# Adding the recurrence's intra-chunk output once per pair of heads instead of after each of the last two steps

## The chip, the cores and the metric

The kernel runs on one core of a Trainium2 chip. A core has a matrix engine (TensorE; the profile writes PE for its matmuls and PEld for its weight loads, which run beside them), a vector engine (VectorE, DVE), a scalar engine (ScalarE, ACT), GpSimd (POOL) and a queue engine for transfers (SP). Matmuls write to PSUM, a small memory of eight banks per partition, each of 512 float32 values; VectorE and ScalarE read it from there into SBUF, the large on-chip memory. The metric is the device time of one execution in microseconds; less is better.

## The reference, cut to what matters

The program is one layer of a hybrid encoder for two sequences of 256 tokens each, 2048 wide: a projection, eight heads of neighbourhood attention, eight heads of a bidirectional gated delta rule, an output projection, a gated MLP and norms. The change lies in the delta rule's recurrence. For one direction and chunks of 64 tokens it is:

```python
def step(S, inp):
    q_i, k_i, u_i, w_i, g_i, qk_i = inp
    v_new = u_i - jnp.einsum('bhcd,bhde->bhce', w_i, S)
    o = jnp.einsum('bhcd,bhde->bhce', q_i * jnp.exp(g_i)[..., None], S) \
        + jnp.einsum('bhcs,bhse->bhce', qk_i, v_new)
    g_last = g_i[..., -1]
    S = S * jnp.exp(g_last)[..., None, None] + jnp.einsum(
        'bhcd,bhce->bhde', k_i * jnp.exp(g_last[..., None] - g_i)[..., None], v_new)
    return S, o
...
o = o_fwd + o_bwd
o = o * lax.rsqrt(jnp.mean(o * o, axis=-1, keepdims=True) + RMS_EPS) * norm_w.astype(jnp.float32)
o = o * jax.nn.silu(heads(z).astype(jnp.float32))
```

So a chunk's output has two summands: the state part (the query times the state S) and the part inside the chunk (`qk_i` times `v_new`). Four chunks follow each other in each direction, and the outputs of both directions are added.

## The kernel before

**Stages.** The 512 tokens of both sequences go through together, with features on the 128 partitions. First the kernel computes the projections head by head: GEMM tiles of 128 columns by 512 tokens, each in two halves (`half_gemm`), each half with a weight tile of 128x1024 that is loaded by SP's queue and split in two by `split` (`w_hi` on ScalarE, line 138, `w_lo` on VectorE, line 139). One half is 24 matmuls. Then come the output projection, and the MLP as blocks of smaller products (`block`, from line 1090), which take more than half of the time, and the last norm.

**Chains beside the GEMM stream.** Attention and recurrence are written as Python generators and stand in the lists `chains` and `side`. Within a `half_gemm`, `pump()` is called after every two k-slices (six matmuls) and drives the first generator of each list to its next `yield`. A chain thus puts its few matmuls into the GEMM stream at fixed places; `pause(n)` leaves n such places empty, so that other engines have time.

**What sets the order.** All TensorE instructions are pinned in the order in which the program issues them (`mm` and `transpose`, lines 86 to 90), and so are some others (`pin`). The order of the rest on VectorE, ScalarE and the queues is laid out by the framework's planner, by priority, which follows the place in the program; `tc.high_priority(offset=AHEAD)` moves the weights' splits 120 places forward. The framework also sets all waits between engines. Each engine works through its own queue in order.

**The recurrence.** Heads go in pairs. `recur_pair(h)` waits for both heads' preparation, takes two PSUM tiles `O[0]` and `O[1]` (one bank each, tags o0 and o1), and drives `recur(h, O)` and `recur(h + 1, O)` in turns through `together`: at each place in the stream both heads do the same piece, head h first. `O[hf]` is seen as (i, q, e): head of the pair, one of two positions `pp`, and 128 features; its partitions are two halves of 64, one for each sequence. Both heads of a pair, and both positions, therefore lie in the same two tiles.

**The four steps.** A head's loop over `st` (line 796) takes one chunk in each direction per step: the chunks at position `pp` = 0 in steps 0 and 3, at `pp` = 1 in steps 1 and 2. A step consists of
- from step 1 on: the state's products with key and query (line 811, into `pks`), the right side `rv` on VectorE (line 815), and the state part of the output, scaled, into the SBUF tile `os_` (line 820 on VectorE in step 2, line 822 on ScalarE in steps 1 and 3);
- the solve (line 827) and its copy `n` (line 829, ScalarE);
- up to step 2: the new state, products at line 838 into `pS`, then scaled and added up by VectorE (line 849), or copied by ScalarE in step 0 (line 843);
- the part inside the chunk: four matmuls into `O[0]` and `O[1]` (line 855; the trace shows them as ps_o, eight records per head). They accumulate over the two steps with the same `pp`, so that `O` is complete for `pp` = 1 behind step 2 and for `pp` = 0 behind step 3;
- in steps 2 and 3: VectorE adds `O` to `os_`, one add of 128x128 for each of the two tiles (line 860).

**The end of a pair.** `recur_pair` appends `finish_pair(h)` to `side`. Its squares (line 881, eight per pair on ScalarE, each with a row sum) read `os_`; small operations on VectorE make the norm's factor from them (lines 885 to 887), four multiplications scale `os_` (line 891), and after `FIN_GAP` = 5 places TensorE transposes `os_` (line 902; recorded in the helper's line 90 as ps_s<-ident,os). VectorE then multiplies by the gate (line 908), and `split` writes `dmix`, the output projection's input.

**The next pair.** `prepare` of the next pair waits until both heads are in `traced`, fetches their arrays (`fetch`: a load of `kq` on SP's queue and four of `uq` on POOL's, into buffers that the earlier pair's ps_o matmuls have read), and transposes `kq` and `v` through PSUM tiles of a ring of three (`sm_tile`); ScalarE's copy at line 781 (`dvn`) and VectorE's products at line 786 (`kd`) make these free.

Of the kernel before, what the change touches and what calls it, by code (L numbers as in the profile page):

```python
# [13 lines left out]
ALU = mybir.AluOpType  # L14
# [60 lines left out]
def hybrid_encoder(ctx: ExitStack, tc: tile.TileContext, xT, w_in, w_ba, w_out, w_gate,  # L75
# [4 lines left out]
    tt = nc.vector.tensor_tensor  # L80
# [5 lines left out]
    def mm(*a, **k):  # L86
        pin(nc.tensor.matmul(*a, **k))  # L87

    def transpose(*a):
        pin(nc.tensor.transpose(*a))  # L90
# [67 lines left out]
    def newton_rsqrt(out, x, pool):  # L158

        a = pool.tile(list(x.shape), F32, tag="nw", bufs=2, name="nw")  # L160
        ai, oi = a.bitcast(I32), out.bitcast(I32)
        ts(ai, x.bitcast(I32), 1, None, ALU.logical_shift_right)
        ts(oi, ai, -1, 0x5f3759df, ALU.mult, ALU.add)
        for _ in range(3):
            stt(a, out, -0.5, x, ALU.mult, ALU.mult)
            tt(a, a, out, ALU.mult)
            stt(out, a, 1.5, out, ALU.add, ALU.mult)
# [20 lines left out]
    def together(*gens):  # L188

        gens = list(gens)  # L190
        while gens:
            turn = gens[:]
            while turn:
                said = [(g, next(g, DONE)) for g in turn]
                gens = [g for g in gens if (g, DONE) not in said]
                turn = [g for g, v in said if v == LEVEL]
            if gens:
                yield

    def pause(n):  # L200
        for _ in range(n):
            yield
# [36 lines left out]
    def sm_tile():  # L239
        return psm.tile([P, T], F32, tag="s", name="ps_s")  # L240
# [101 lines left out]
    def ranged(ap, pp):  # L342

        a = ap.rearrange("p (b c t) -> p b c t", b=NB, c=4)
        return a[:, :, 0:4:3] if pp == 0 else a[:, :, 1:3]
# [405 lines left out]
    prepared, outputs, gate, traced, finished = {}, {}, {}, set(), set()  # L751
# [39 lines left out]
    def recur(h, O):  # L791
        dr = state["dr"]
        uq, kq, vn, kd = prepared[h]
        os_ = na.tile([P, 2, NB, P], F32, tag="bias", bufs=2, name="os")
        S = None
        for st in range(4):
            pp = 0 if st in (0, 3) else 1

            dirs = (0, 1) if st < 2 else (1, 0)
            if S is None:  # L800
                rv = vn[:, :, pp]
            else:
                yield from pause(S_GAP)

                pks = sm_tile().rearrange("p (w b e) -> p w b e", w=2, b=NB)
                for w in range(2):
                    for hf in range(2):
                        for b in range(NB):
                            c0 = b * L + pp * P + hf * C
                            to = pks[half[b], 1, hf] if w else pks[half[hf], 0, b]  # L810
                            mm(to, kq[:, w, c0:c0 + C], S[:, dirs[hf], b], start=True, stop=True)
                l0 = h * NB
                rv = dr.tile([P, NB, P], F32, tag=f"r{h % 2}", name="r")
                for b in range(NB):
                    stt(rv[:, b], pks[:, 0, b], egk[:, st, l0 + b:l0 + b + 1], vn[:, b, pp],
                        ALU.mult, ALU.add)
                for hf in range(2):
                    eq = egq[:, LN[hf, st] // 16, h:h + 1]
                    if st == 2:
                        stt(os_[:, pp, hf], pks[:, 1, hf], eq, os_[:, pp, hf], ALU.mult, ALU.add)  # L820
                    else:
                        act(out=os_[:, pp, hf], in_=pks[:, 1, hf], func=AF.Copy, scale=eq)
                yield from pause(R_GAP)
            pn = sm_tile()
            pn3 = pn.rearrange("p (w b e) -> p w b e", w=2, b=NB)[:, 0]
            for b in range(NB):
                mm(pn3[:, b], uq[b][:, st, 0], rv[:, b], start=True, stop=True)
            n = dr.tile([P, NB, P], F32, tag=f"n{h % 2}", name="n")
            nc.scalar.copy(n, pn3)
            yield from pause(N_GAP)  # L830
            if st < 3:
                pS = [None, None]
                for hf in range(2):
                    t = sm_tile() if hf else pg.tile([P, T], F32, tag="g", name="ps_s")
                    pS[dirs[hf]] = t[:, :2 * P].rearrange("p (b e) -> p b e", b=NB)
                for b in range(NB):
                    for hf in range(2):
                        mm(pS[dirs[hf]][:, b], kd[half[hf], st, b], n[half[hf], b],
                           start=True, stop=True)
                Sn = dr.tile([P, 2, NB, P], F32, tag=f"S{h % 2}", bufs=2, name="S")  # L840
                if S is None:
                    for d in range(2):
                        nc.scalar.copy(Sn[:, d], pS[d])
                else:
                    for d in range(2):
                        ch = st if d == 0 else 3 - st
                        for b in range(NB):
                            lane = d * 64 + ch * 16 + h * NB + b
                            stt(Sn[:, d, b], S[:, d, b], egl[:, lane:lane + 1], pS[d][:, b],  # L849
                                ALU.mult, ALU.add)  # L850
                S = Sn
                yield LEVEL
            for b in range(NB):
                for hf in range(2):
                    mm(O[hf][half[b], h % 2, pp], uq[b][half[hf], st, 1, hf * C:hf * C + C],
                       n[half[hf], b], start=(st == 0 and h % 2 == 0), stop=(st > 1),
                       skip_group_check=True)
            if st > 1:
                for hf in range(2):
                    tt(os_[:, pp, hf], os_[:, pp, hf], O[hf][:, h % 2, pp], ALU.add)  # L860
        traced.add(h)
        outputs[h] = os_

    def recur_pair(h):
        while not {h, h + 1} <= set(prepared):
            yield
        yield from pause(CORE_START)
        O = [pso.tile([P, T], F32, tag=f"o{hf}", name="ps_o")
             .rearrange("p (i q e) -> p i q e", i=2, q=2) for hf in range(2)]
        yield from together(recur(h, O), recur(h + 1, O))  # L870
        side.append(finish_pair(h))

    def finish_pair(h):
        dr, dmix = state["dr"], state["dmix"]

        ssq = dr.tile([P, 2, 2, NB], F32, tag="ssq", bufs=2, name="ssq")
        yo = na.tile([P, T], F32, tag="pT", name="yo")
        for i in range(2):
            for pp in (1, 0):
                for hf in range(2):  # L880
                    act(out=yo[:, :P], in_=outputs[h + i][:, pp, hf], func=AF.Square,
                        scale=rqs[:, pp, hf, h + i:h + i + 1], accum_out=ssq[:, i, pp, hf:hf + 1])
        yield
        rs = dr.tile([P, 2, 2, NB], F32, tag="rs", bufs=2, name="rs_o")
        ts(ssq, ssq, 1.0 / P, EPS, ALU.mult, ALU.add)
        newton_rsqrt(rs, ssq, dr)
        tt(ssq, rs, rqs[:, :, :, h:h + 2].rearrange("p q f i -> p i q f"), ALU.mult)
        for i in range(2):
            for pp in (1, 0):
                os_ = outputs[h + i]  # L890
                tt(os_[:, pp], os_[:, pp], ssq[:, i, pp, :, None].broadcast_to([P, NB, P]),
                   ALU.mult)
        yield from pause(FIN_GAP)
        while h + 1 not in gate:
            yield
        pos = []
        for i in range(2):
            po = sm_tile()
            to = po.rearrange("p (b q f c) -> p q f b c", b=NB, q=2, f=2)
            for pp in range(2):  # L900
                for hf in range(2):
                    transpose(to[:, pp, hf], outputs[h + i][:, pp, hf], ident)
            pos.append(po.rearrange("p (b q t) -> p b q t", b=NB, q=2))
        for i in range(2):
            if i:
                yo = na.tile([P, T], F32, tag="pT", name="yo")
            for pp in range(2):
                tt(ranged(yo, pp), pos[i][:, :, pp].rearrange("p b (c t) -> p b c t", c=2),
                   ranged(gate[h + i], pp), ALU.mult)
            split(dmix[:, 0, h + i], dmix[:, 1, h + i], yo, dnw)  # L910
            finished.add(h + i)
# [76 lines left out]
    st = st_cm.__enter__()  # L988
# [475 lines left out]
```

## Time and profile before

| | |
|---|---|
| runs | 2266.14, 2270.9, 2271.24 us; median 2270.9 us |
| profiled execution | 2266.53 us; its span 2264.7 us |
| busy in the span | PE 2240.1 us, DVE 1777.8 us, ACT 1031.8 us, POOL 236.6 us |
| mean granted TensorE clock | 0.997 of full speed |
| chain that ended last | PE 93%, DVE 4%, DMA 1%, issue 1% |
| the added line 860 | 32 adds of 128x128, first at 567.7 us, last at 787.9 us |
| transfers | 381.21 MB, mean 168 GB/s |

The profile is taken by the hardware on one execution, in microseconds from the start of the span. A group's row gives line, engine, operation, output<-inputs, shapes and count, then the busy time in us and the mean time of one in ns, then the engine's idle time ahead of the group and what ended it. A row of the order of time gives start, duration, line, operation and count, with the idle time ahead of it and what ended that in brackets; instructions of one kind that stand together are merged, and the count is that of all. A row of the list of waits gives who waited for whom, the sum in us, how often, and the longest. Matmuls overlap, and their ends are modelled, so the start of the next weight load tells more of the pace than a matmul's duration. "issue" is idle time for which the profile shows no releaser. A wait for several things is put down to the one that came last.

### The profile page before, as it was taken

What the parts mean: (1) busy time and instruction counts of PE and PEld (TensorE: products, weight loads), DVE (VectorE), ACT (ScalarE), POOL (GpSimd) and SP (SyncE); (2) the same over time, 40 slices, a digit from 0 to 9 for tenths busy, and PEclk for the clock granted to TensorE, in tenths of its full rate; (3) what the DMA queues carried; (4) which work ended last, traced back from release to release, by engine and by line L of the source; (5) the groups of instructions that cost most, each with busy time, mean ns of one, the idle gap of its engine ahead of it and who ended that gap; (6) DMA issues with size and microseconds to landing.
All of it is one profiled execution on the core that took longest, in us unless ns stands there. A gap on an engine that the chain in (4) does not pass through costs nothing.

```text
span 2264.7 us, 32764 instructions
## 1 busy us (share of the span) xinstructions
PE 2240.1 (99%) x12436; PEld 1914.7 (85%) x12436; DVE 1777.8 (79%) x2742; ACT 1031.8 (46%) x1552; POOL 236.6 (10%) x370
## 2 busy tenths in 40 slices
PE   9999999999999999999999999999999999999998
PEld 7888888888777788888888888888888888888888
DVE  7954799964555546898888888888888798998966
ACT  6564433333433425654444444444444464444435
POOL 1321000010000010101111110110110001001010
PEclk9999999999999999999999999999999999999999
DMA  5344322263333455777777777777777477667672
GB/s 209 130 139 149 109 98 94 100 154 117 103 103 94 178 184 177 214 196 203 206 187 211 198 214 203 207 196 210 198 192 195 143 195 198 177 180 203 181 204 84
DMA packets 112542, 381.21 MB, mean 168 GB/s; under 512 B 14049, under 2 KB 14641, under 8 KB 112129
## 3 DMA queue, kind: packets, MB, share of 16 engines
q1 hardware_dynamic: 77552, 266.25, 35.0%
q0 software_dynamic: 33680, 110.78, 23.4%
q8 instruction: 98, 1.61, 0.3%
q10 hardware_dynamic: 1152, 2.10, 0.3%
q14 instruction: 60, 0.48, 0.1%
HBM read 343.66 MB, written 35.41 MB: 167 GB/s over the span
## 4 chain that ended last, share of the span: by engine, by line
PE 93%; DVE 4%; DMA 1%; issue 1%; ACT 0%; POOL 0%; SPq 0%; DVEq 0%; ACTq 0%; POOLq 0%
PE ps_g L87 35%; PE ps_c L87 14%; PE ps_d L87 14%; PE ps_a L87 14%; PE ps_b L87 7%; PE ps_s L87 7%; DVE prod L590 1%; PE ps_s L90 1%; DVE w_lo L139 1%; DVE W L592 1%; DMA kkq<-s_gram 1%; PE ps_o L87 0%; PE ps_e L87 0%; DVE cacc L357 0%; DVE S L849 0%
## 5 line engine op out<-in xcount | busy, mean ns | idle before, releaser
L87 PE MATMUL ps_g<-xhi,w_hi 128*128 128x512 f32 x880 | 353.0, 401 | 0.0
L87 PE MATMUL ps_g<-xhi,w_lo 128*128 128x512 f32 x880 | 344.2, 391 | 0.7 <-DVE w_lo L139 0.7
L87 PE MATMUL ps_g<-xlo,w_hi 128*128 128x512 f32 x880 | 344.2, 391 | 0.3 <-DVE xlo L257 0.3
L138 ACT ACTIVATE w_hi<-w_raw 128x1024 fp32r<-128x1024 f32 x164 | 173.4, 1058 | 280.5 <-PE ps_g L87 219.9
L138 ACT ACTIVATE w_hi<-b 128x1024 fp32r<-128x1024 f32 (+1 forms) x180 | 185.8, 1032 | 239.0 <-issue 120.0
L139 DVE TENSOR_TENSOR w_lo<-w_raw,w_hi 128x1024 fp32r<-128x1024 f32 x164 | 200.1, 1220 | 110.5 <-ACT w_hi L138 103.6
L138 ACT ACTIVATE w_hi<-w_first 128x1024 fp32r<-128x1024 f32 (+1 forms) x180 | 185.4, 1030 | 180.3 <-PE ps_c L87 90.8
L139 DVE TENSOR_TENSOR w_lo<-w_first,w_hi 128x1024 fp32r<-128x1024 f32 (+1 forms) x180 | 213.6, 1187 | 59.9 <-ACT w_hi L138 56.3
L139 DVE TENSOR_TENSOR w_lo<-b,w_hi 128x1024 fp32r<-128x1024 f32 (+1 forms) x180 | 212.9, 1183 | 7.7 <-ACT w_hi L138 7.2
L87 PEld LDWEIGHTS ps_g<-xhi,w_hi 128*128 128x128 f32 x880 | 166.0, 189 | 38.3 <-issue 5.3
L87 PEld LDWEIGHTS ps_g<-xhi,w_lo 128*128 128x128 f32 x880 | 165.9, 189 | 37.1 <-DVE w_lo L139 1.1
L87 PEld LDWEIGHTS ps_g<-xlo,w_hi 128*128 128x128 f32 x880 | 166.2, 189 | 33.6 <-DVE xlo L257 1.1
L87 PE MATMUL ps_d<-xc,w_hi 128*128 128x512 f32 x704 | 175.1, 391 | 0.0
L87 PE MATMUL ps_c<-xc,w_hi 128*128 128x512 f32 x704 | 175.1, 391 | 0.0
L87 PE MATMUL ps_a<-xc,w_hi 128*128 128x512 f32 x696 | 173.1, 391 | 0.0
L87 PEld LDWEIGHTS ps_c<-xc,w_hi 128*128 128x128 f32 x704 | 129.4, 188 | 25.0
L87 PEld LDWEIGHTS ps_d<-xc,w_hi 128*128 128x128 f32 x704 | 129.3, 188 | 25.0
L87 PEld LDWEIGHTS ps_a<-xc,w_hi 128*128 128x128 f32 x696 | 127.9, 188 | 24.8
L138 ACT ACTIVATE w_hi<-w_second 128x1024 fp32r<-128x1024 f32 (+1 forms) x60 | 62.0, 1034 | 92.9 <-DVE ga L1158 50.3
L87 PE MATMUL ps_d<-xc,w_lo 128*128 128x256 f32 x704 | 98.5, 283 | 0.0
L87 PE MATMUL ps_c<-xc,w_lo 128*128 128x256 f32 x704 | 98.5, 283 | 0.0
L87 PE MATMUL ps_a<-xc,w_lo 128*128 128x256 f32 x696 | 97.4, 283 | 0.0
(391 smaller groups left out, 4199.2 us busy)
## 6 DMA issues: line engine op xcount, KB each, us to landing
w_raw<-in_w_in_dram SPq DMA_DIRECT2D x108, 512.0 KB, 3.3
b<-in_w_gate_dram SPq DMA_DIRECT2D x66, 512.0 KB, 4.1
b<-in_w_up_dram SPq DMA_DIRECT2D x66, 512.0 KB, 4.9
b<-in_w_group_dram SPq DMA_DIRECT2D x48, 448.0 KB, 4.2
w_raw<-in_w_out_dram SPq DMA_DIRECT2D x32, 512.0 KB, 3.5
w_raw<-in_w_down_dram SPq DMA_DIRECT2D x24, 512.0 KB, 3.7
w_second<-in_w_gate_dram SPq DMA_DIRECT2D x22, 512.0 KB, 7.3
w_first<-in_w_gate_dram SPq DMA_DIRECT2D x22, 512.0 KB, 4.6
```

The source lines that it names most:

```text
L87: pin(nc.tensor.matmul(*a, **k))
L90: pin(nc.tensor.transpose(*a))
L138: act(out=hi, in_=src, func=AF.Copy)
L139: tt(lo, src, r32(hi), ALU.subtract)
L590: stt(pv, W[:, s0:s1, s0:c], ndm[:, c:c + 1], kkq[:, c, 0, None, s0:c].broadcast_to([P, n, j]), ALU.mult, ALU.mult)
L592: nc.vector.tensor_reduce(W[:, s0:s1, c], pv, AX.X, ALU.add)
```

## The change

The adds at line 860 leave the loop. `recur_pair` does them behind `together`, once both heads have done all four steps: one add for each head and tile, over both positions, so four of 128x256 per pair instead of eight of 128x128. What is computed stays the same, and so do the matmuls with their order, their accumulation flags, and all places at which a generator yields.

```diff
@@ -855,9 +855,6 @@
                     mm(O[hf][half[b], h % 2, pp], uq[b][half[hf], st, 1, hf * C:hf * C + C],
                        n[half[hf], b], start=(st == 0 and h % 2 == 0), stop=(st > 1),
                        skip_group_check=True)
-            if st > 1:
-                for hf in range(2):
-                    tt(os_[:, pp, hf], os_[:, pp, hf], O[hf][:, h % 2, pp], ALU.add)
         traced.add(h)
         outputs[h] = os_
 
@@ -868,6 +865,10 @@
         O = [pso.tile([P, T], F32, tag=f"o{hf}", name="ps_o")
              .rearrange("p (i q e) -> p i q e", i=2, q=2) for hf in range(2)]
         yield from together(recur(h, O), recur(h + 1, O))
+        for i in range(2):
+            for hf in range(2):
+                os_ = outputs[h + i][:, :, hf]
+                tt(os_, os_, O[hf][:, i], ALU.add)
         side.append(finish_pair(h))
 
     def finish_pair(h):
```

## The prediction

> **What bounds the kernel now.** I read the page first (span, busy times), then the two halves of TensorE's wait list, then the group row of the added line, then the busy times by stage.
>
> ```profile
> span 2264.7 us, 32764 instructions
> PE 2240.1 (99%) x12436; PEld 1914.7 (85%) x12436; DVE 1777.8 (79%) x2742; ACT 1031.8 (46%) x1552; POOL 236.6 (10%) x370
> ```
> ```profile
> PE ps_o L87 <- DVE os L860: 11.9, 9, 3.0
> ...
> PE ps_d L87 <- DVE p L1145: 0.5, 1, 0.5
> ```
> ```profile
> PEld ps_o L87 <- DVE os L860: 10.2, 5, 3.2
> ```
> ```profile
> L860 DVE TENSOR_TENSOR os<-os,ps_o 128x128 f32<-128x128 f32 x32 | 7.9, 282 | 10.1 <-PE ps_o L87 10.1
> ```
> ```profile
> 520.00:800.00 280.00, 268.06 (x1867) 216.98 (x1866) 152.21 (x364) 102.18 (x230) 18.50 (x28) 0.99 0.37 117
> ...
> 950.00:2200.00 1250.00, 1249.52 (x7012) 1095.96 (x7011) 1088.67 (x1442) 586.94 (x715) 124.51 (x157) 1.00 0.72 196
> ```
>
> In the last fence the columns are the stretch, its length, the busy time of PE, PEld, DVE, ACT and POOL, the granted clock, the DMA share and GB/s. TensorE is busy 2240.1 of 2264.7 us, so only about 25 us of the span can be won by taking waits away. Almost half of that is one kind of wait: TensorE stands at the recurrence's output matmuls (ps_o) until the add of line 860 is done. The recurrence runs between 520 and 800 us, and that is the stretch where TensorE isn't full (268.06 of 280). Behind it, in the FFN stage, PE is full (1249.52 of 1250), so what is won there should arrive at the end.
>
> The two wait rows, 11.9 us for matmuls and 10.2 us for weight loads, are two views of the same stalls and aren't added. To size a stall I go to the order of time on the weight-load side (start, duration, name, count, and in brackets the idle time before it). The first row is a step without an add, the others the second head's half of the eight steps with one (four pairs, steps 2 and 3).
>
> ```profile
> 551.39 0.43 PEld L87 LDWEIGHTS ps_o<-n,uq 64*64 64x64 f32 x16
> ...
> 568.03 0.40 PEld L87 LDWEIGHTS ps_o<-n,uq 64*64 64x64 f32 x8 [1.85 <-DVE os L860]
> ...
> 582.45 0.34 PEld L87 LDWEIGHTS ps_o<-n,uq 64*64 64x64 f32 x8 [0.75 <-issue]
> ...
> 640.91 0.40 PEld L87 LDWEIGHTS ps_o<-n,uq 64*64 64x64 f32 x8 [3.24 <-DVE os L860]
> ...
> 656.92 0.34 PEld L87 LDWEIGHTS ps_o<-n,uq 64*64 64x64 f32 x8 [0.75 <-ACT dvT L361]
> ...
> 706.58 0.49 PEld L87 LDWEIGHTS ps_o<-n,uq 64*64 64x64 f32 x8 [2.65 <-DVE os L860]
> ...
> 723.19 0.19 PEld L87 LDWEIGHTS ps_o<-n,uq 64*64 64x64 f32 x2 [1.59 <-issue]
> 723.99 0.20 PEld L87 LDWEIGHTS ps_o<-n,uq 64*64 64x64 f32 x6 [0.61 <-DVE os L860]
> ...
> 772.72 0.40 PEld L87 LDWEIGHTS ps_o<-n,uq 64*64 64x64 f32 x8 [1.85 <-DVE os L860]
> ...
> 787.10 0.33 PEld L87 LDWEIGHTS ps_o<-n,uq 64*64 64x64 f32 x8 [0.70 <-issue]
> ```
>
> Both heads of a pair write into the same two PSUM tiles, O[0] and O[1]. Without an add, both heads' loads run through in 0.43 us. With one, the second head's loads wait until the vector engine has read the first head's part of the tile, although the columns differ: the dependency goes by the tile. At 640.91 the add itself was late, since it stood in VectorE's queue behind the state update and a weight split.
>
> **The change part by part.** *Removed: the add between the two heads.* Both heads finish in the same turn of `together`, so the 16 loads of a step now stand in TensorE's order with no reader between them, as in the row of 551.39. Each stall is worth its idle time, plus what the second half takes above 0.21 us (half of 0.43), since it also waits for the second tile's add. By row: 1.85+0.19, 0.75+0.13, 3.24+0.19, 0.75+0.13, 2.65+0.28, 1.59+0.61+0.18, 1.85+0.19 and 0.70+0.12 make 15.4 us. Where a row names "issue" or dvT as the releaser I still count it: the step has the same order, and the 0.75 us are about what an add of 0.28 us needs with the matmul before it and the way back.
>
> *Removed with it: a slower TensorE behind the longest stalls.* The chain of waits shows the 18 GEMM matmuls that follow the output matmuls:
>
> ```profile
> 568.68 4.31 PE ps_g L87 x18
> ...
> 641.55 5.90 PE ps_g L87 x18
> ...
> 707.48 5.40 PE ps_g L87 x18
> ```
> ```profile
> 642.00:646.00 4.00, 4.00 (x13) 3.13 (x12) 0.08 (x1) 0.00 (x0) 0.00 (x0) 0.64 0.32 116
> ```
>
> Behind the stalls of 3.24 and 2.65 us the same 18 matmuls take 5.90 and 5.40 us in place of 4.31, and the granted clock in 642 to 646 is 0.64. Behind a stall of 1.85 us nothing of that is seen. That is 1.59 + 1.09 = 2.7 us more, so the stalls are worth 18.1 us together. The Trainium skill (TensorE: Matmul & The Clock Gate, "What's actually happening") has the clock halved after an idle window of about 3.4 us. No idle time here is that long, so by that page the 2.7 us would not hang on these stalls and the sum would be 2.7 us smaller. The granted clock behind the two stalls says they do, and I go by it.
>
> *Moved: the adds, to behind the last step.* Eight adds of 128x128 per pair become four of 128x256. Line 1060 adds the same size from PSUM:
>
> ```profile
> L1060 DVE TENSOR_TENSOR p<-p,ps_a 128x256 f32<-128x256 f32 x60 | 24.7, 412 | 0.0
> ```
>
> Four by 0.41 us is 1.65 us in place of 8 by 0.28 = 2.26. VectorE isn't what TensorE waits for in this stage (152.21 of 280 us), so the 0.6 us is worth nothing. No DMA is issued by the moved step. The fetch of the next pair waits on POOL's queue for ps_o matmuls and not for the adds, so it moves with TensorE. The next pair's first write to O comes only behind that pair's preparation, long after the last add.
>
> *What now comes later: the finishing chain.* Its squares read what the adds write. Before, two of a pair's eight squares ran as early as step 2; now none can start before the merged adds. First pair, last step:
>
> ```profile
> 582.05 0.48 DVE L860 TENSOR_TENSOR os<-os,ps_o 128x128 f32<-128x128 f32 x2 [3.38 <-PE ps_o L87]
> ```
> ```profile
> 568.02 0.40 ACT L881 ACTIVATE yo<-os,rqs 128x128 f32<-128x128 f32 x1 [2.19 <-DVE os L860]
> ...
> 582.37 0.40 ACT L881 ACTIVATE yo<-os,rqs 128x128 f32<-128x128 f32 x1 [3.15 <-DVE os L860]
> ...
> 582.90 0.40 ACT L881 ACTIVATE yo<-os,rqs 128x128 f32<-128x128 f32 x1
> ...
> 584.42 1.06 ACT L138 ACTIVATE w_hi<-w_raw 128x1024 fp32r<-128x1024 f32 x1
> ...
> 586.21 0.19 ACT L881 ACTIVATION_READ_ACCUMULATOR yo<-os,rqs 128x1 f32 x1
> ```
> ```profile
> 585.51 1.22 DVE L139 TENSOR_TENSOR w_lo<-w_raw,w_hi 128x1024 fp32r<-128x1024 f32 x1 [1.93 <-ACT w_hi L138]
> 586.66 0.26 DVE L885 TENSOR_SCALAR ssq<-ssq 128x8 f32<-128x8 f32 x1
> ...
> 589.38 1.43 DVE L891 TENSOR_TENSOR os<-os,ssq 128x256 f32<-128x256 f32 x4
> ```
> ```profile
> 591.03 1.02 PEld L90 LDWEIGHTS ps_s<-ident,os 128*128 128x128 f32 x8
> ```
>
> The first merged add waits 0.21 us longer (the other head's matmuls) and takes 0.41 in place of 0.28, so the first square starts at 582.71. Eight squares at 0.53 us (582.37 to 582.90) and the w_hi between them (0.96 us net) end at about 587.9, 1.5 us later than now (586.40). L885 stands behind w_lo today (to 586.73), so it moves by 1.2 us. Head h's scaled output is then ready at 591.3 (now 590.1, half of the four L891) and head h+1's at 592.0. TensorE's order isn't changed, and this step has lost 0.88 us, so it arrives at the transposes at 590.15 and not at 591.03. It waits 1.2 us for the first four and 0.2 us more for the second four: 1.4 us. Behind the waiting transposes stands the GEMM stream. The fourth pair has the same shape:
>
> ```profile
> 793.93 1.43 DVE L891 TENSOR_TENSOR os<-os,ssq 128x256 f32<-128x256 f32 x4
> ```
> ```profile
> 795.70 1.02 PEld L90 LDWEIGHTS ps_s<-ident,os 128*128 128x128 f32 x8
> ```
>
> By the same shift (1.2 us later, TensorE 0.82 us earlier) it waits 1.3 us. The second and third pair have room, since their transposes stand behind the next pair's preparation:
>
> ```profile
> 668.44 0.41 DVE L891 TENSOR_TENSOR os<-os,ssq 128x256 f32<-128x256 f32 x1
> ```
> ```profile
> 677.15 1.03 PE L90 MATMUL ps_s<-ident,os 128*128 128x128 f32 x8
> ```
>
> 8.3 us lie between. But there the added squares stand ahead of the copy dvn on ACT, which frees the PSUM slot that the last of the preparation's transposes need:
>
> ```profile
> 729.51 0.57 ACT L781 COPY dvn<-ps_s 128x512 f32<-128x512 f32 x1
> ```
> ```profile
> 731.26 0.60 PE L90 MATMUL ps_s<-ident,kq 128*128 128x128 f32 x4
> ```
>
> The copy ends 1.18 us before these. TensorE comes 2.38 us earlier (the third pair's step 3). If ACT doesn't come earlier at all, that costs 1.2 us; if the copy moves along, nothing. I take the middle, 0.6.
>
> *Sum.* 18.1 − 1.4 − 1.3 − 0.6 = 14.8 us. Bounds of the give-back: 0, if the planner puts the w_hi behind the squares and the small operations ahead of w_lo, and about 15 us (the second rival).
>
> The profiled execution took 2266.5 us (its span of 2264.7 and 1.8 around it), 4.4 us less than the median of 2270.9. I sum against the middle of the two, 2268.7: the forecast is 2253.9, say **2254 us**.
>
> **The rivals.** *No give-back.* The chain keeps pace, because ACT and VectorE get the squares and small operations in a better order: 2268.7 − 18.1 = 2250.6. For it: w_hi and w_lo stand in the chain's way today without being urgent. Against: two more squares behind the adds are 1.05 us, and the free time ahead of the transposes is only 0.9 us for head h.
>
> *The chain becomes the new wait.* If the planner puts two more weight tiles' splits (1.06 + 1.22 us each) ahead of the squares and the small operations, the first and fourth pair's transposes come 4.6 us later still. Two stalls of about 5.9 us, each with a clock loss of about 1.3 us as seen above, and the 0.6 give back 15 us: 3.1 us are left, 2265.6, not to be told from no change. For it: VectorE's and ACT's orders come from a planner that sets weight splits ahead. Against: in these rows only one split stands inside the chain. The Trainium skill speaks for this side (Perfetto Trace Analysis, "Optimizing Scalar/DVE Operations"): where such an engine isn't full and still makes others wait, cutting instructions smaller may let work end sooner, and this change does the opposite. That the adds go on holding TensorE between the heads is excluded, since all four now need both heads.
>
> *Slower: the plan changes elsewhere.* With fewer instructions ahead, and at other times, the planner may order VectorE and ACT otherwise in the FFN stage, where VectorE is 1088.67 of 1250 us busy. The place is the block's subtraction from ps_d (line 1145):
>
> ```profile
> L1145 DVE TENSOR_TENSOR p<-ps_d,p 128x512 f32<-128x512 f32 x60 | 41.0, 683 | 0.1
> ```
>
> It made TensorE wait once, for 0.5 us. If that came in each of the 60 blocks, it would cost 30 us: 2253.9 + 30 = 2284. From 14.8/60 = 0.25 us a block on it eats the gain, from 0.36 on it is slower by over 0.3%. For it: VectorE's small reserve. Against: nothing of that stage is touched, and it starts at about 950 us, well behind the last pair.
>
> **How the numbers follow.** Forecast 0.64, no give-back 0.12, chain as the new wait 0.12, slower 0.12. What a measurement of this kernel tells from no change is about 0.3%, 6.8 us. Forecast and first rival are faster by more: 0.76. The second is within: 0.12. The third is slower: 0.12. The low end is the first rival against the profiled time (2248.4) with a microsecond for a smaller clock loss elsewhere: 2247. The high end takes in the second rival against the shown median (2270.9 − 3.1): 2268. Left out is the slower case.
>
> **What would show it.** Right: no ps_o wait for an add in TensorE's list; all output matmuls of a step through in about 0.43 us on the load side; no 18 GEMM matmuls over 4.4 us behind them, and a granted clock near 1 around 640 and 710; L860 gone, four 128x256 adds per pair near 0.41 us, eight squares behind each last step; short waits of TensorE for the scaled output at the first and fourth pair only. Wrong: waits of several microseconds at these transposes (second rival); new waits for VectorE behind 950 us (third); or the stretch from 520 to 800 shorter and the end not earlier.

## The result, and the profile after

| | before | after |
|---|---|---|
| median of the runs compared | 2269.61 us (6 runs, 2266.14 to 2271.24) | 2254.18 us (6 runs, 2253.19 to 2255.89) |
| profiled execution | 2266.53 us, span 2264.7 us | 2254.44 us, span 2252.7 us |
| matmuls, VectorE and ScalarE instructions | 12436, 2742, 1552 | 12436, 2726, 1552 |

The ratio is 0.9934, with a 95% interval of 0.9921 to 0.9947: the change makes the kernel 0.5 to 0.8% faster. Between the profiled executions it is 12.0 us of span, between the medians 15.4 us; why these differ is a result of its own (below). One of the five runs of the first variant below took 3172.94 us at a mean granted clock of 0.654, a slow run that its median counts and its ratio leaves out.

TensorE's list of waits after, whole rows; the wait for line 860 is gone, and a new one heads the list (line numbers behind the added lines are one higher, line 871 holds the merged adds):

```profile
PE ps_s L90 <- DVE os L892: 2.9, 2, 2.2
...
PE ps_d L87 <- DVE p L1146: 0.5, 1, 0.5
...
PE ps_s L90 <- ACT dvn L781: 0.3, 1, 0.3
...
PE ps_g L87 <- DVE S L849: 0.2, 1, 0.2
```

The weight loads in order of time, after: step 2 of the first and second pair, step 3 of the second to fourth, and the transposes of the first and fourth pair.

```profile
566.08 0.42 PEld L87 LDWEIGHTS ps_o<-n,uq 64*64 64x64 f32 x16
566.91 0.19 PEld L87 LDWEIGHTS ps_g<-xhi,w_hi 128*128 128x128 f32 x1 [0.41 <-DVE S L849]
...
589.57 0.42 PEld L90 LDWEIGHTS ps_s<-ident,os 128*128 128x128 f32 x4 [1.14 <-issue]
590.24 0.42 PEld L90 LDWEIGHTS ps_s<-ident,os 128*128 128x128 f32 x4 [0.25 <-PE ps_s L90]
...
597.03 0.46 PEld L90 LDWEIGHTS ps_s<-ident,dvT 128*128 128x128 f32 x4 [0.18 <-ACT dvn L781]
597.87 0.42 PEld L90 LDWEIGHTS ps_s<-ident,kq 128*128 128x128 f32 x4 [0.38 <-DVE yo L909]
...
636.47 0.43 PEld L87 LDWEIGHTS ps_o<-n,uq 64*64 64x64 f32 x16
...
649.96 0.43 PEld L87 LDWEIGHTS ps_o<-n,uq 64*64 64x64 f32 x16 [0.35 <-issue]
...
710.34 0.43 PEld L87 LDWEIGHTS ps_o<-n,uq 64*64 64x64 f32 x16 [0.35 <-issue]
...
770.73 0.42 PEld L87 LDWEIGHTS ps_o<-n,uq 64*64 64x64 f32 x16 [0.35 <-issue]
...
781.94 0.42 PEld L90 LDWEIGHTS ps_s<-ident,os 128*128 128x128 f32 x4 [2.58 <-issue]
782.61 0.42 PEld L90 LDWEIGHTS ps_s<-ident,os 128*128 128x128 f32 x4 [0.25 <-PE ps_s L90]
```

Where two rows of eight with an idle time between them stood before, one row of 16 stands now. In front of the scaled output's transposes TensorE now waits, 1.1 us at the first pair and 2.6 us at the fourth. Right behind the latter the clock is halved for one stretch:

```profile
783.20:786.60 3.40, 3.40 (x10) 2.62 (x9) 1.70 (x4) 1.43 (x2) 0.00 (x0) 0.50 0.47 192
```

A measure that leaves the start and the FFN out is the time from the recurrence's first matmul to the FFN's first. In the order of time, before and then after:

```profile
531.76 0.53 PEld L87 LDWEIGHTS ps_s<-dvn,uq 128*128 128x128 f32 x3
...
942.11 0.19 PEld L87 LDWEIGHTS ps_a<-xc,w_hi 128*128 128x128 f32 x1
```
```profile
531.87 0.41 PEld L87 LDWEIGHTS ps_s<-dvn,uq 128*128 128x128 f32 x2
...
930.01 0.41 PEld L87 LDWEIGHTS ps_a<-xc,w_hi 128*128 128x128 f32 x2
```

That is 410.35 and 398.14 us: all of the 12 us lie here. What follows takes the same time in both (from these starts to the end of the span 1322.6 and 1322.7 us), so nothing of it is lost in the FFN. I call this time the middle stretch and give it for every run, together with the number of half-clock stretches that the trace has in it (3.4 us each, but for one of twice that length in the last row):

| run | middle stretch, us | half-clock stretches |
|---|---|---|
| before; again; a third time | 410.35; 412.17; 410.42 | 2; 3; 2 |
| the change; again | 398.14; 398.15 | 1; 1 |
| adds per step, behind both heads; again | 392.65; 392.68 | 0; 0 |
| step 3 alone | 407.46 | 3 |
| step 2 alone | 397.35 | 0 |
| change, transposes later | 394.49 | 0 |
| change, small adds | 398.01 | 1 |
| change, transposes of two pairs later | 392.39 | 0 |
| before, each add three times | 422.89 | 5, one of them 6.8 us long |

### The profile page after: what moved, and what is told of

It is laid out like the page before. It is cut to its first block, busy times and chain, and to the rows that moved or that the text cites. A ratio compares the mean times of both kernels' runs of the same rounds, so it can differ in the third digit from the quotient of the medians.

```text
span 2252.7 us, 32733 instructions
## 1 busy us (share of the span) xinstructions
PE 2236.2 (99%) x12436; PEld 1912.0 (85%) x12436; DVE 1776.4 (79%) x2726; ACT 1031.8 (46%) x1552; POOL 237.2 (11%) x370
## 4 chain that ended last, share of the span: by engine, by line
PE 91%; DVE 5%; DMA 2%; ACT 1%; issue 1%; POOL 0%; SPq 0%; DVEq 0%; ACTq 0%; POOLq 0%
PE ps_g L87 33%; PE ps_c L87 14%; PE ps_d L87 14%; PE ps_a L87 14%; PE ps_b L87 7%; PE ps_s L87 7%; DVE w_lo L139 1%; DMA w_raw<-in_w_in_dram 1%; DVE prod L590 1%; DVE W L592 1%; PE ps_s L90 1%; DMA kkq<-s_gram 1%; PE ps_o L87 0%; ACT w_hi L138 0%; PE ps_e L87 0%
```

## The experiments

The theory was: TensorE's wait between the heads is the whole gain, and what is given back is its wait for a finishing chain that starts later. The rivals: fewer and larger adds are the gain; the last step alone counts; the lost time lies in the planner's order elsewhere.

**Adds per step, but behind both heads.** `LEVEL` hands the turn to the other head within the same place of the stream.

```diff
             if st > 1:
+                yield LEVEL
                 for hf in range(2):
                     tt(os_[:, pp, hf], os_[:, pp, hf], O[hf][:, h % 2, pp], ALU.add)
```

> The adds stay in the loop (32 of 128x128, in steps 2 and 3), but each step's adds come behind the output matmuls of both heads. Theory (TensorE's wait between the heads is the whole gain, the late finishing chain the give-back): all eight stalls gone as with the change, no 18 GEMM matmuls over 4.4 us, and of the give-back (5.8 us in the profile of the change) only 0 to 1.5 us, since two squares per pair run early again: span 2247 to 2249 us, that is 4 to 6 us under the change's 2252.7. Rival 1 (the gain comes from fewer, larger adds on VectorE): near the kernel before, 2262 to 2265. Rival 2 (the gain needs the last step's merge): between, 2252 to 2258.

Measured: span 2248.5 us, median 2249.79 us, ratio to the kernel before 0.9913 (0.9897 to 0.9928). Between 500 and 900 us TensorE's list of waits is this one row:

```profile
PE ps_g L87 <- DVE S L849: 0.2, 1, 0.2
```

So no matmul waits at the transposes, and the middle stretch is 17.7 us shorter than before. All 32 small adds are still there, so their number and size are not the gain; their place is.

> The adds per step, behind both heads, again. Theory: no wait of TensorE over 0.5 us between 520 and 800 us, so no clock loss that could differ from run to run: 2248.5 to 2250.5 us in all runs, scatter under 1.5 us, 3 to 5 us under the changed kernel in the same comparison. Rival (the gap seen before is chance): within 1.5 us of it.

Measured in another comparison: span 2247.7 us, median 2249.73 us, runs from 2249.45 to 2250.01; ratio 0.9907 (0.9894 to 0.9921). One wait of 0.6 us, a little more than expected, lies at 528 us in the first pair's preparation, ahead of the recurrence. The change itself, beside it:

> The changed kernel as it is, beside the next run and on the same chip. Theory: 1 to 4 us behind the run with the adds per step behind both heads; two stretches of TensorE's wait at the transposes, first and fourth pair. The clock loss behind the fourth pair's wait of about 2.6 us may be there or not (it was, 1.6 us, in the profile of the change): span 2251 to 2253.5.

Measured: span 2252.9 us, median 2253.71 us, ratio 0.9926 (0.9913 to 0.994). The waits at the transposes are those of the first profile to the hundredth. The per-step place is 4.0 us better by the medians, and the middle stretch, the same within 0.03 us in two profiles of each, says 5.5 us. The intervals of the two ratios just overlap, but the runs of the two don't (2253.07 to 2255.84 us here against 2249.45 to 2250.01), so the lead rests on the runs of this comparison and on the traces.

**One step alone.** The same `yield LEVEL`, in step 3 or in step 2 alone:

```diff
             if st > 1:
+                if st == 3:
+                    yield LEVEL
                 for hf in range(2):
```

> Only step 3's adds come behind both heads; step 2's stay between the heads. Theory: step 3's four stalls (0.88+0.88+2.38+0.82 = 5.0 us) go, step 2's (13 us with the clock loss) stay, 0 to 1 us given back at the transposes: span about 2260.4 us (2259.5 to 2261.5). Rival (step 3 counts for all, since the finishing hangs on it): as much as the change, 2252 to 2254.

Measured: span 2262.4 us, out of the expected range; median 2264.2 us, ratio 0.998 (0.9971 to 0.9989). Its waits are as expected, four at step 2:

```profile
PE ps_o L87 <- DVE os L862: 8.6, 4, 3.0
```

But the clock fell behind three of them, not two. In the chain of waits, the 18 GEMM matmuls behind the first pair's step 2, which took 4.31 us in the first profile of before:

```profile
569.48 5.65 PE ps_g L87 x18
```

Less that one more stretch (1.7 us), the middle stretch is 4.6 us shorter than before, against 5.0 us of stalls.

> Only step 2's adds come behind both heads; step 3 stays as before. Theory: step 2's stalls and both clock losses go (2.04+3.43+2.93+2.04+2.7 = 13.1 us, 0.2 us back for the state update that frees the GEMM's PSUM tile), nothing is given back at the transposes: span about 2251.8 us (2251 to 2253). With the run for step 3 it should add up to the run with both. Rival (the stalls of step 3 alone matter, or step 2's are made up elsewhere): 2260 to 2265.

Measured: span 2253.3 us, 0.3 us past the range; median 2254.56 us, ratio 0.9936 (0.9924 to 0.9949). The middle stretch is 13.0 us shorter, as summed; the recurrence starts 1.5 us later than in the first profile of before, and that is the miss. The step-3 waits stay:

```profile
PE ps_o L87 <- DVE os L862: 3.3, 5, 1.4
```

Both steps count, and with the one more half-clock stretch of the step-3 run taken off they add up: 13.0 + 4.6 = 17.6 against 17.7 with both.

**Where the give-back lies.** The changed kernel, with the transposes two places later in TensorE's order:

```diff
-FIN_GAP = 5
+FIN_GAP = 7
```

> The changed kernel with FIN_GAP 7 in place of 5: the transposes of the scaled output stand two places (12 GEMM matmuls, some 2.8 us) later in TensorE's order. Theory: the change's give-back is TensorE's wait at these transposes and the clock loss behind the fourth pair's (2.6 us wait, 1.6 us slower matmuls); both vanish, and the GEMM matmuls behind the fourth pair run at full clock: span 2252.7 - 5.5 = 2247 us (2246.5 to 2248.5). Rival (the time is lost to the planner's order or at the end of the stage): no change, 2252 to 2254, or more where the next pair's preparation, two places later, is now awaited.

Measured: span 2250.6 us, median 2250.72 us, ratio 0.9921 (0.9908 to 0.9933). Half a miss: the waits at the first and fourth pair and the half-clock stretch are gone, but the second and third pair have a new one:

```profile
678.90 0.42 PEld L90 LDWEIGHTS ps_s<-ident,os 128*128 128x128 f32 x4 [0.95 <-ACT os L822]
...
740.51 0.66 PE L90 MATMUL ps_s<-ident,os 128*128 128x128 f32 x4 [1.00 <-ACT os L822]
```

There the moved transposes came between the next pair's state products and the scaling that frees one of the ring's three PSUM tiles. So the pause was lengthened for the two pairs that need it:

```diff
-        yield from pause(FIN_GAP)
+        yield from pause(FIN_GAP + 2 * (h in (0, 6)))
```

> The changed kernel with the transposes two places later for the first and the fourth pair alone (FIN_GAP + 2 there). Theory: the four-pair variant won the waits of these two pairs and lost 2.2 us at the second and third pair, where the moved transposes met the next recurrence in the ring of three PSUM tiles; without these it is as good as the adds per step behind both heads: span 2247 to 2248.5, runs 2249 to 2250.5, no half-clock stretch between 500 and 900 us. Rival (the give-back has another cause): 2250 or more.

Measured: span 2247.0 us, median 2248.92 us (2248.58 to 2249.35), ratio 0.9899 (0.9884 to 0.9914). No wait for the scaled output is left, and the middle stretch is 392.39 us, 5.75 under the change: the whole give-back. This and the adds per step are the two best versions; their intervals don't separate them.

**Size of the adds.** The changed kernel, with eight small adds in the same place:

```diff
+            for pp in (1, 0):
                 for hf in range(2):
-                    os_ = outputs[h + i][:, :, hf]
-                    tt(os_, os_, O[hf][:, i], ALU.add)
+                    os_ = outputs[h + i][:, pp, hf]
+                    tt(os_, os_, O[hf][:, i, pp], ALU.add)
```

> The changed kernel, but with eight adds of 128x128 behind the last step instead of four of 128x256. Theory (place counts, size doesn't): within 1 us of the changed kernel, 2252 to 2255; the added 0.6 us of VectorE time per pair delays the finishing by at most that. Rival (merging saves time): 2 us or more slower than the changed kernel.

Measured: median 2254.1 us, ratio 0.9928 (0.9915 to 0.994), middle stretch 398.01 us against 398.14. Merging is worth nothing here.

**More of the suspected cost.** The kernel before, with each add done as add, subtract, add:

```diff
                 for hf in range(2):
-                    tt(os_[:, pp, hf], os_[:, pp, hf], O[hf][:, h % 2, pp], ALU.add)
+                    for op in (ALU.add, ALU.subtract, ALU.add):
+                        tt(os_[:, pp, hf], os_[:, pp, hf], O[hf][:, h % 2, pp], op)
```

> The kernel before, but each add between the heads done as add, subtract, add, so that O is read three times as long; one output rounding differs. Theory: per step the second head's matmuls wait 0.4 to 1 us longer, eight times, 3 to 8 us in all, and with stalls of about 2.5 to 4 us more of them fill half a clock window: 4 to 6 half-clock stretches of 3.4 us, 1.7 us each, in place of two or three. Span 2271 to 2280. Rival (the stalls are hidden by what follows): within 3 us of the kernel before.

Measured: span 2276.8 us, median 2278.83 us, ratio 1.0036 (1.0025 to 1.0048).

```profile
PE ps_o L87 <- DVE os L861: 18.4, 9, 3.2
```
```profile
568.50:571.90 3.40, 3.40 (x14) 2.56 (x15) 2.98 (x9) 1.27 (x5) 0.00 (x0) 0.50 0.32 108
```

The wait grows from 11.9 to 18.4 us, which is 6.5 us. Five half-clock stretches (the first is shown) stand in place of two, and the fourth, from 728.9 us on, is 6.8 us long, so the clock is low for 13.7 us more. At half clock that costs up to 6.8 us, somewhat less since TensorE also waits within the long stretch. The middle stretch grew by 12.5 us against these 13.3 at most: the stalls are paid about in full.

**The kernel before, profiled again.**

> The kernel before, profiled once more. Its runs go from 2265.3 to 2272.9 us. Theory: the stalls are the same in each execution, and what differs is behind how many of them the clock drops; each costs 1.1 to 1.9 us of slower GEMM matmuls. In this profile the idle times at the second head's output matmuls agree with the first profile's within 0.1 us, and the count of 18-matmul stretches over 5 us behind them, two in the first profile, goes with the time: two near 2266, three near 2268, four or more at 2270 and above. Rival (the scatter lies elsewhere, DMA or start): the same two stretches whatever the time.

Measured: 2270.0 us, span 2268.2 us. The idle times at the second head's loads are the first profile's, row by row; three of them:

```profile
569.63 0.40 PEld L87 LDWEIGHTS ps_o<-n,uq 64*64 64x64 f32 x8 [1.85 <-DVE os L860]
...
644.10 0.40 PEld L87 LDWEIGHTS ps_o<-n,uq 64*64 64x64 f32 x8 [3.24 <-DVE os L860]
...
774.58 0.40 PEld L87 LDWEIGHTS ps_o<-n,uq 64*64 64x64 f32 x8 [1.85 <-DVE os L860]
```

But the clock fell elsewhere, behind both stalls of 1.85 us and the third pair's step 3, and not behind the longest. It fell three times, where four or more were expected for a run of 2270 us. Busy times and clock by stretch:

```profile
570.90:574.20 3.30, 3.30 (x10) 2.55 (x9) 2.48 (x6) 0.72 (x1) 0.00 (x0) 0.50 0.43 159
642.50:645.90 3.40, 1.80 (x13) 1.43 (x14) 2.23 (x6) 0.99 (x4) 0.00 (x0) 1.00 0.30 80
724.50:727.80 3.30, 3.30 (x13) 2.46 (x8) 1.89 (x5) 2.79 (x12) 3.30 (x5) 0.50 1.06 264
775.70:779.00 3.30, 3.30 (x9) 2.60 (x8) 0.55 (x3) 0.00 (x0) 0.00 (x0) 0.50 0.50 159
```

> The kernel before, profiled a third time. Theory: the same idle times at the second head's matmuls; the half-clock stretches, each 3.4 us long and a whole number of 3.413 us apart, at another choice of stalls; the span is 2261.3 plus 1.7 us for each of them, within 1.5 us. Rival: the same two stretches as in the first profile.

Measured: 2268.28 us, span 2266.5 us, with two half-clock stretches, behind the same stalls as in the first profile. So the rival came true: the choice of stalls was that of the first profile. The span is 1.8 us over the expected 2264.7, a miss by 0.3 us; the middle stretch (410.42 us) is the first profile's, and the rest lies in front of the recurrence, which starts at 533.41 us instead of 531.76. So the scatter has two sources, and the stretches are one of them: with three the middle takes 1.8 us more. What differs in the first 530 us was not followed up.

## Why the prediction was right, point by point

**The stalls.** All eight went, and the 16 loads of a step run through in 0.42 to 0.43 us, as in the row of 551.39. The 18.1 us of stalls and clock show up as 17.7 us in the variant that gives nothing back. Some 0.2 us went into a wait that the prediction didn't have: behind the first pair's step 2, TensorE now reaches the next GEMM tile before VectorE's state update has freed it (the row of 566.91). It was right to count the rows that name "issue" or dvT: they are most of step 3's stalls, and moving step 3's adds alone brought 4.6 us.

**The clock.** The 2.7 us were right for the profile they were read from. The step "the granted clock behind the two stalls says they do" was too narrow: the drop doesn't belong to those two stalls. In the second profile it followed stalls of 1.85 us and spared the one of 3.24 us. One execution's count of drops was taken for a property of the stalls.

**The give-back.** The first pair was predicted at 1.4 us; its transposes stand 1.1 + 0.1 us (0.25 of idle time where 0.17 is usual after such a group), and two more short idle times of 0.18 and 0.38 us follow on the load side in the next pair's preparation, where the matmuls show no wait. The third pair was put at 0.6 us; nothing is seen there. The mis-sized term is the fourth pair, "by the same shift it waits 1.3 us" (the same working from its rows gives 1.2): it waited 2.6 us, and the half-clock stretch behind it cost another 1.6 or 1.7. The reason is in VectorE's order of time, where the small operations stand between the first row and the scaling by `ssq`. Before, with the row of 793.93:

```profile
791.30 0.17 DVE L885 TENSOR_SCALAR ssq<-ssq 128x8 f32<-128x8 f32 x1
```

After:

```profile
776.94 0.17 DVE L886 TENSOR_SCALAR ssq<-ssq 128x8 f32<-128x8 f32 x1 [1.80 <-ACT yo L882]
...
778.85 0.68 DVE L975 TENSOR_TENSOR h<-h,ps_g 128x512 f32<-128x512 f32 x1
...
779.53 1.22 DVE L139 TENSOR_TENSOR w_lo<-w_raw,w_hi 128x1024 fp32r<-128x1024 f32 x1
...
781.07 1.43 DVE L892 TENSOR_TENSOR os<-os,ssq 128x256 f32<-128x256 f32 x4
```

Before, the small operations took 2.6 us (791.30 to 793.93), and no other work stood between them. Now they take 4.1 us (776.94 to 781.07), since the planner sets the next output-projection add and a whole weight split between them. This is a piece of the second rival, at one pair. Together 5.5 us were given back where 3.3 were summed, and the run with these two pairs' transposes moved wins all of it back: it is the first rival's case, reached by another edit.

**The sum.** 12.2 us of middle stretch against 14.8 predicted. The medians' 15.4 us come closer, since most executions of the kernel before lose more than the first profiled one, by half-clock stretches and, in both later profiles, in the first 530 us. Setting the sum against the middle of profile and median took up part of that. That 2254 and 2254.18 agree so closely is luck: the give-back was 2.2 us larger than summed, and most executions of the kernel before lost more to the clock than the 2.7 us in the sum (24 of its 33 runs beside the variants had a lower granted clock than the first profile's 0.997).

**The adds and the FFN.** Merged adds took 0.416 us each (0.41 was taken):

```profile
L871 DVE TENSOR_TENSOR os<-os,ps_o 128x256 f32<-128x256 f32 x16 | 5.9, 416 | 7.7 <-PE ps_o L87 7.7
```

The time in VectorE was worth nothing, as the run with small adds shows. The slower rival didn't come: TensorE's one wait at the blocks' subtraction is still one of 0.5 us.

## What to carry to other kernels

When two interleaved chains write into one PSUM tile, let both write before either is read: a read of a third of a microsecond between them cost TensorE up to 3 us, since it waits for all that stands ahead of the read in VectorE's queue. Defer the read only past the other writer and not to the end, where it delays the chain that hangs on it; or move the consumer as well. And price a stall of TensorE from several profiles, because the clock drop behind it comes and goes.

## What the runs showed of the hardware

The half-clock stretches between 500 and 960 us are 3.413 us long, but for one of twice that length, and stand on a fixed grid within an execution: in the second profile of before they begin at 570.9, 724.5 and 775.7 us, 45 and 15 times 3.413 us apart. What decides seems to be how long the matmuls were busy in the window before. In that profile the stall of 3.24 us (640.86 to 644.10) was cut by a window's end at about 642.5 and left the matmuls busy for 1.96 and 1.86 us in the two windows, while the one of 1.85 us fell whole into the window that ends at 570.9 and left 1.80. The thirteen traces, cut along their grids from 10 to 2200 us, agree: in the 18 windows right before a new half-clock stretch the matmuls were busy for 0.51 to 1.80 us, and in no other window at full clock for less than 1.80 us. The Trainium skill (TensorE: Matmul & The Clock Gate, "What's actually happening") has such a free-running window of 3413 ns, which these traces agree with. It names an idle window as the condition; here windows in which the matmuls were busy for up to 1.80 us were enough. No run was made to find the limit, and the ends of matmuls are modelled, so 1.80 us is a reading of these traces alone.

A stall's price therefore has a part that depends on where it falls, from 0 to 1.7 us, which explains part of the before kernel's scatter (2265.3 to 2274.1 us in all of its runs). The mean granted clock of its 33 runs beside the variants goes with the time: the nine at 0.997 took 2265.3 to 2268.6 us, the seven at 0.994 took 2271.5 to 2274.1. The versions without long stalls scatter less, by 0.6 to 1.7 us (the adds per step, twice, and the transposes of two pairs later).

That TensorE waits for a read of other columns in the same tile is seen in every profile of before. The Trainium skill (PSUM — Partial Sum Buffer, "PSUM bank collisions raise a hardware error") says that two engines at one bank and the same 32 partitions collide whatever the columns, so the framework's wait has a reason; no run here tried to go without it. Tiles of its own for each head, the other way to take the read out from between the writers, were not tried either.
